# Merging two mask products, reading tokens from PSUM, moving a division to GpSimd, and giving a scheduler the flag `port_shared` and one higher cost figure, in a hybrid attention layer

## The chip, the cores and the metric

The kernel runs on the 8 cores of one Trainium2 chip (two dies, cores 0 to 3 and 4 to 7). Each core does the whole layer for 2048 of the 16384 tokens. The metric is the device time of the slowest core in microseconds (us). Runs come in states: a slow state with one or both dies at a lower clock is left out of every comparison. The span is first to last instruction.

## The reference

One decoder layer: attention in three dilated groups and a pooled branch, both gated and merged, one output projection, then a gated feed-forward. The parts that the change touches:

```python
h = rms_norm(x, g_pre_mix); proj = h @ w_in          # q, k, v, u (256 wide), gates
q, k = apply_rope(q), apply_rope(k)
# per group (window, dilation) = (128,1), (512,4), (2048,16), four heads of 64 each:
p = where(valid, exp(s - m), 0); den = sum(p); out = (p @ v) / den    # banded mask
# the groups are combined by their denominators: o = sum(num_g) / sum(den_g)
# pooled branch, group g of 64 channels, windows 2, 4, 8, 16:
z = trailing_sum(u, w) / count - u                    # mean minus the token itself
y_pool = (z @ w_mix[g]) * scale
merged = gate_a * (o_attn @ w_proj_attn) + gate_p * (y_pool @ w_proj_pool)
x = x + rms_norm(merged @ w_out, ...)
# feed-forward: silu(h2 @ w_gate) * (h2 @ w_up) @ w_down, residual, about half of the time
```

## The kernel before

The kernel records its operations as nodes. A list scheduler in the host program then fixes the order of every engine before anything runs: it simulates the engines with a cost per operation, lets an engine take the ready operation with the best priority, and assigns buffers from rings as it goes.

The cost of a GpSimd operation, and the point at which a node may start:

```python
def op_cost(eng, method, outs, ins, kw):
    ...                                    # TensorE, ScalarE, VectorE cut
    return 0.17 + (0.0034 if strided else 0.0021) * n      # GpSimd, n elements a partition

def earliest(self, n):
    t = n.ready
    if n.dma:
        t = max(t, self.dma_free - self.BACKLOG)
    ...                                    # places in buffer rings cut
    return t
```

One tile of scores, for two heads: TensorE, exponential on ScalarE, then a mask product on VectorE for each head (128x512, bf16, both inputs in SBUF). There are 48 such tiles and two buffers for them (`PT`).

```python
def att_qk(pair, items, mask):
    pt, sb = PT.new(), sc2.new()
    ...                                    # matmuls into sb
    act.activation(out=pt[:, :, :], in_=sb[:, :, :], func=AF.Exp, scale=0.125)
    for hh in range(2):
        dve.tensor_tensor(out=pt[:, hh, :], in0=pt[:, hh, :], in1=masks[:, mask, :], op=ALU.mult)
    return pt
```

The end of an attention block, for each of four token blocks and two head pairs: numerators `val` and denominators `den` come from PSUM, the reciprocal is an exponential of minus a logarithm, and VectorE multiplies:

```python
for o_, i_, hh in ((val[lo, :], lo, 0), (val[hi, :], hi, 1), (den[lo, :], hi, 0), (den[hi, :], lo, 1)):
    dve.tensor_tensor(out=o_, in0=ob[i_, hh, :], in1=acc[i_, s, 2 * pair + hh, :], op=ALU.add)
act.activation(out=den[:, :], in_=den[:, :], func=AF.Ln)
act.activation(out=den[:, :], in_=den[:, :], func=AF.Exp, scale=-1.0)
dve.tensor_tensor(out=oT2[...] rearranged, in0=val[...], in1=den[...], op=ALU.mult)
```

The pooled branch: the token values go from PSUM into an SBUF buffer `uX`, in front of which the last 16 columns of the block before are copied; GpSimd builds trailing sums by shifted additions; VectorE scales them and subtracts the token:

```python
for c in range(2):
    X = uX[c]
    dve.tensor_copy(out=X[:, 0:16], in_=uh[:, c, :] if s == 0 else X[:, 512:528])
    b = r1.new()                                   # one PSUM bank of the filling ring
    mm8(b[:, :], ...)
    act.activation(out=X[:, 16:UL], in_=b[:, :], func=AF.Copy)
for c in range(2):
    X = uX[c]
    shift_add(uY, X, 1); shift_add(uZ, uY, 2)      # GpSimd; two more when c == 1
    for p0, Sx in ((0, uY), (64, uZ)):
        p = slice(p0, p0 + 64)
        dve.scalar_tensor_tensor(out=zT[p, :], in0=Sx[p, 16:UL], scalar=invw[p, c:c + 1],
                                 in1=X[p, 16:UL], op0=ALU.mult, op1=ALU.subtract)
        ...                                        # first 16 columns of block 0 cut
```

GpSimd also does the rotary embedding's additions (`q`, `k` from the products `rt`, which VectorE forms with one operand in PSUM) and issues weight transfers. Meanwhile TensorE fills its time between attention tiles with the projections of the next block.

The softmax here doesn't subtract the row's maximum and nothing guards it: scores larger than these inputs give would overflow.

Of the kernel before, what the change touches and what calls it, by code (L numbers as in the profile page):

```python
# [8 lines left out]
AF = mybir.ActivationFunctionType  # L9
# [96 lines left out]
class Node:  # L106
    __slots__ = ("idx", "eng", "items", "outs", "ins", "deps", "succ", "cost", "prio", "dma", "sem", "vts", "start", "finish", "tick", "nin", "ready", "table", "prev")
# [17 lines left out]
class Eng:  # L125
# [16 lines left out]
    def call(self, method, *args, after=(), **kw):  # L142
        n = self.open
        if n is None:
            n = self.prog.node(self)
        outs, ins = [], []
        for i, a in enumerate(args):
            if isinstance(a, (bass.AP, VAP)):
                (outs if i == 0 else ins).append(a)
        for k, a in kw.items():  # L150
            if isinstance(a, (bass.AP, VAP)):
                (outs if k in ("out", "accum_out") else ins).append(a)
        n.items.append((method, args, kw))
        n.outs += outs
        n.ins += ins
        n.deps.update(a.idx for a in after if a is not None)
        n.cost += op_cost(self.name, method, outs, ins, kw)
        if method == "activation":
            t = TABLES.get(kw["func"])
            if t:  # L160
                n.table = t
        if self.open is None:
            self.prog.close(n)
        return n
# [61 lines left out]
def op_cost(eng, method, outs, ins, kw):  # L226
# [21 lines left out]
    return 0.17 + (0.0034 if strided else 0.0021) * n  # L248


class Prog:
# [42 lines left out]
    def node(self, eng):  # L294
        n = Node()
        n.idx = len(self.nodes)
        n.eng = eng
        n.items, n.outs, n.ins = [], [], []
        n.deps, n.succ = set(), []
        n.cost, n.dma, n.sem, n.table = 0.0, 0, None, None  # L300
        n.prio = n.idx + self.bias
        n.vts = []
        self.nodes.append(n)
        return n
# [140 lines left out]
    def earliest(self, n):  # L445
        t = n.ready
        if n.dma:
# [10 lines left out]
    def schedule(self):  # L458
# [13 lines left out]
        self.dma_free = 0.0  # L472
        self.order = []
        import bisect
        while len(self.order) < len(nodes):
# [39 lines left out]
            e.free = t + cost  # L515
            if n.dma:
# [128 lines left out]
def build_program():  # L645
# [292 lines left out]
    for d, w in todo:  # L938
        pool.dma(d, w, dsem("d_w01_"), after=[sp_x[-1]])
# [16 lines left out]
    def att_qk(pair, items, mask):  # L956
# [9 lines left out]
        for hh in range(2):  # L966
            dve.tensor_tensor(out=pt[:, hh, :], in0=pt[:, hh, :], in1=masks[:, mask, :], op=ALU.mult)
# [39 lines left out]
    def att(s):  # L1007
# [40 lines left out]
        for pair in range(2):  # L1048
# [7 lines left out]
            for o_, i_, hh in ((val[lo, :], lo, 0), (val[hi, :], hi, 1), (den[lo, :], hi, 0), (den[hi, :], lo, 1)):  # L1056
# [4 lines left out]
            dve.tensor_tensor(out=oT2[s % 3][:, pair, :].rearrange("p (j rho) -> p rho j", rho=4), in0=val[:, :].rearrange("p (rho j) -> p rho j", rho=4),  # L1061
                              in1=den[:, :].rearrange("p (rho j) -> p rho j", rho=4), op=ALU.mult)


    def pooled(s, r1):
        for c in range(2):
            X = uX[c]
            dve.tensor_copy(out=X[:, 0:16], in_=uh[:, c, :] if s == 0 else X[:, 512:528])
            b = r1.new()
            mm8(b[:, :], lambda k: wu[:, c, k, :], lambda k: hT[:, k, s * 512:(s + 1) * 512])  # L1070
            act.activation(out=X[:, 16:UL], in_=b[:, :], func=AF.Copy)

# [3 lines left out]
        for c in range(2):  # L1076
            X = uX[c]
            shift_add(uY, X, 1)
# [4 lines left out]
            for p0, Sx in ((0, uY), (64, uZ)):  # L1083
                p = slice(p0, p0 + 64)
                dve.scalar_tensor_tensor(out=zT[p, :], in0=Sx[p, 16:UL], scalar=invw[p, c:c + 1], in1=X[p, 16:UL], op0=ALU.mult, op1=ALU.subtract)
                if s == 0:
                    dve.tensor_tensor(out=Sx[p, 16:32], in0=Sx[p, 16:32], in1=invc[p, 16 * c:16 * c + 16], op=ALU.mult)
                    dve.tensor_tensor(out=zT[p, 0:16], in0=Sx[p, 16:32], in1=X[p, 16:32], op=ALU.subtract)
# [223 lines left out]
```

## Time and profile before

| | before |
|---|---|
| timed, median of 3 (range) | 1035.83 us (1034.78 to 1103.5) |
| profiled span, slowest core | 1022.7 us |
| TensorE / VectorE / GpSimd busy | 930.7 / 420.4 / 352.7 us |

I split the span by what TensorE does: up to its first attention scores; from there to the first gate matmul of the merge; from there to the first feed-forward matmul; the rest. Busy times by stretch, kernel before, core 5 (start and end; length, then busy time and instructions of TensorE, its weight loads, VectorE, ScalarE and GpSimd; granted clock; DMA share; GB/s):

```profile
0.00:149.20 149.20, 113.36 (x832) 76.11 (x832) 87.96 (x143) 85.30 (x160) 66.99 (x55) 0.95 0.71 189
149.20:308.00 158.80, 139.88 (x1390) 87.00 (x1390) 134.79 (x188) 80.54 (x109) 76.67 (x51) 0.97 0.21 39
308.00:547.60 239.60, 220.14 (x1165) 101.46 (x1164) 110.47 (x134) 103.32 (x157) 123.97 (x136) 0.98 0.46 109
547.60:1022.70 475.10, 457.35 (x2140) 207.91 (x2136) 87.23 (x109) 77.26 (x131) 85.07 (x109) 0.99 0.43 93
```

The length less TensorE's busy time is its gap: 35.8, 18.9, 19.5 and 17.8 us, 92 us in all. In the second stretch VectorE is busy for 134.8 of 158.8 us.

### The profile page before, as it was taken

How to read it: one execution, taken by the hardware profiler on the slowest of the kernel's cores; microseconds unless marked ns; L12 is line 12 of the kernel's file. 1: busy time of each engine (PE TensorE's matmuls, PEld its weight loads, DVE VectorE, ACT ScalarE, POOL GpSimd, SP SyncE). 2: the span in 40 equal slices, each digit the busy share in tenths (PEclk: the TensorE clock that was granted, in tenths of full speed). 3: DMA queues.
4: the chain of work that ended last, by engine and by line, in shares of the span. 5: the costliest groups of instructions: out<-in, count | busy, mean ns of one | idle time of the engine just before them, and what ended most of it. 6: DMA issues, size and time to landing. Idle time of an engine off the chain costs nothing.

```text
span 1022.7 us, 15344 instructions; the slowest of 8 cores (1018.5 to 1022.7 us)
## 1 busy us (share of the span) xinstructions
PE 930.7 (91%) x5520; PEld 472.5 (46%) x5520; DVE 420.4 (41%) x573; ACT 346.4 (34%) x556; POOL 352.7 (34%) x350
## 2 busy tenths in 40 slices
PE   2779898989787988999989999999999999999993
PEld 2346585556453443444444444444444444444441
DVE  5668448679998343433455211211112121121111
ACT  4686437645343242422766111111101111111110
POOL 1528445344757512333886110111332000001232
PEclk9899999999999989999999999999999999999997
DMA  8868711220061635331777667663323444430321
GB/s 234 261 188 217 172 30 43 31 54 1 1 114 22 99 59 121 62 62 22 208 263 225 117 116 124 119 109 62 124 104 122 83 79 69 80 62 1 124 83 41
DMA packets 30778, 105.02 MB, mean 103 GB/s; under 512 B 3952, under 2 KB 3952, under 8 KB 30704
## 3 DMA queue, kind: packets, MB, share of 16 engines
q0 software_dynamic: 14432, 45.65, 26.9%
q1 hardware_dynamic: 15984, 58.33, 17.1%
q8 instruction: 45, 0.74, 0.3%
q14 instruction: 29, 0.24, 0.1%
q10 hardware_dynamic: 288, 0.06, 0.1%
HBM read 132.90 MB, written 16.78 MB: 146 GB/s over the span
## 4 chain that ended last, share of the span: by engine, by line
PE 72%; DVE 9%; issue 7%; POOL 6%; ACT 5%; DMA 1%; DVEq 0%; POOLq 0%; ACTq 0%; SPq 0%
PE ps L596 63%; PE ps L594 9%; DVE PT_75_117 L594 2%; ACT xsb_53_95 L594 1%; DVE PT_74_116 L594 1%; DVE rt_72_114 L594 1%; DVE zT_134 L594 1%; DVE rt_73_115 L594 1%; DMA xst_37_79<-xo 1%; POOL x1b_101_143 L594 1%; POOL x1b_102_144 L594 1%; DVE hTh_69 L594 1%; POOL x1b_103_145 L594 1%; ACT junk_55_97 L594 1%; ACT PT_75_117 L594 0%
## 5 line engine op out<-in xcount | busy, mean ns | idle before, releaser
L596 PE MATMUL ps<-wdna_155,ffT_154 128*128 128x512 bf16 x512 | 115.7, 379 | 0.0
L596 PE MATMUL ps<-hT_68,wgu_109_151 128*128 128x512 bf16 x420 | 100.4, 379 | 0.0
L596 PE MATMUL ps<-hT_68,wgu_110_152 128*128 128x512 bf16 x420 | 100.4, 379 | 0.0
L596 PE MATMUL ps<-hT_68,wgu_111_153 128*128 128x512 bf16 x392 | 93.7, 379 | 0.0
L596 PEld LDWEIGHTS ps<-wdna_155,ffT_154 128*128 128x128 bf16 x512 | 50.1, 98 | 60.4
L596 PEld LDWEIGHTS ps<-hT_68,wgu_109_151 128*128 128x128 bf16 x420 | 41.0, 98 | 49.3
L596 PEld LDWEIGHTS ps<-hT_68,wgu_110_152 128*128 128x128 bf16 x420 | 41.0, 98 | 49.1
L596 PEld LDWEIGHTS ps<-hT_68,wgu_111_153 128*128 128x128 bf16 x392 | 38.4, 98 | 46.2
L596 PE MATMUL ps<-hT_68,wgs_76_118 128*128 128x512 bf16 x224 | 56.3, 393 | 2.9 <-ACT tg_80_122 L594 1.8
L596 PE MATMUL ps<-hT_68,wgs_77_119 128*128 128x512 bf16 x224 | 53.5, 379 | 2.1 <-ACT tg_81_123 L594 1.0
L594 DVE TENSOR_TENSOR ffT_154<-ps,sa_115_157 128x512 bf16<-128x512 f32 x30 | 20.7, 691 | 79.2 <-PE ps L594 79.2
L594 DVE TENSOR_TENSOR ffT_154<-ps,sa_116_158 128x512 bf16<-128x512 f32 x29 | 20.1, 692 | 78.4 <-PE ps L594 78.4
L594 DVE TENSOR_TENSOR ffT_154<-ps,sa_117_159 128x512 bf16<-128x512 f32 x29 | 20.1, 691 | 77.1 <-PE ps L594 77.1
L594 ACT ACTIVATE sa_115_157<-ps 128x512 f32<-128x512 f32 x30 | 17.9, 598 | 80.1 <-PE ps L594 80.1
L594 ACT ACTIVATE sa_116_158<-ps 128x512 f32<-128x512 f32 x29 | 17.3, 597 | 80.8 <-PE ps L594 80.8
L594 ACT ACTIVATE sa_117_159<-ps 128x512 f32<-128x512 f32 x29 | 17.3, 597 | 78.0 <-PE ps L594 78.0
L594 DVE TENSOR_TENSOR PT_75_117<-PT_75_117,masks_44 128x512 bf16<-128x512 bf16 x48 | 39.6, 864 | 8.6 <-ACT PT_75_117 L594 8.5
L594 ACT ACTIVATE junkd_107_149<-ps 128x1024 bf16<-128x1024 f32 x18 | 18.3, 1016 | 73.2 <-PE ps L594 73.1
L594 DVE SCALAR_TENSOR_TENSOR tg_80_122<-tg_80_122,ps 128x512 f32<-128x512 f32 x32 | 22.0, 689 | 46.8 <-ACT tg_80_122 L594 44.1
L596 PE MATMUL ps<-wdnb_156,ffT_154 128*128 128x512 bf16 x160 | 39.8, 379 | 0.0
L594 DVE SCALAR_TENSOR_TENSOR tg_81_123<-tg_81_123,ps 128x512 f32<-128x512 f32 x32 | 22.0, 687 | 40.4 <-ACT tg_81_123 L594 40.3
L594 ACT ACTIVATE junkd_108_150<-ps 128x1024 bf16<-128x1024 f32 x14 | 14.2, 1017 | 69.4 <-PE ps L594 69.4
(499 smaller groups left out, 1821.6 us busy)
## 6 DMA issues: line engine op xcount, KB each, us to landing
wgu_109_151<-wgu POOLq DMA_DIRECT2D x15, 512.0 KB, 5.8
wgu_110_152<-wgu POOLq DMA_DIRECT2D x15, 512.0 KB, 5.8
wgu_111_153<-wgu POOLq DMA_DIRECT2D x14, 512.0 KB, 5.7
wgs_76_118<-wg POOLq DMA_DIRECT2D x8, 512.0 KB, 5.3
wgs_77_119<-wg POOLq DMA_DIRECT2D x8, 512.0 KB, 6.1
wdna_155<-wdn POOLq DMA_DIRECT2D x8, 512.0 KB, 8.6
tab_70_112<-tab SPq DMA_DIRECT2D x6, 512.0 KB, 6.0
tab_71_113<-tab SPq DMA_DIRECT2D x6, 512.0 KB, 6.1
```

The lines of the kernel that those rows point to most:

```text
L594: e.ops.append(lambda q, m=method, a=a, k=k, s=sem.sem, v=step: getattr(q, m)(*a, **k).then_inc(s, v))
L596: e.ops.append(lambda q, m=method, a=a, k=k: getattr(q, m)(*a, **k))
```

## The change

The intent: take work off VectorE in the attention stage, keep it out of GpSimd's way, and let the scheduler know that a GpSimd instruction and a VectorE instruction with two inputs in SBUF hold each other up. In the trace of the kernel before, core 5, a VectorE multiply of this form took 4.88 us beside two GpSimd additions and 1.30 us with GpSimd idle; a rotary addition of GpSimd took up to 2.88 us beside such VectorE instructions, and at most 2.17 us beside those that read one operand from PSUM. "Shared port" is my name for this, in the diff and below; the traces show the waiting, not a port. One cost figure of the scheduler changes as well, that of GpSimd operations on rearranged data.

```diff
+def port_shared(eng, outs, ins):
+    return eng == "vector" and sum(not type(peek(a).tensor).__name__.startswith("PSum") and nelem(peek(a)) > 1 for a in ins) > 1
 ...
-    return 0.17 + (0.0034 if strided else 0.0021) * n
+    return 0.17 + (0.0040 if strided else 0.0021) * n
 ... # in earliest(); port_free is set when such a VectorE node is placed
+        if n.port:
+            t = max(t, self.pool.free)
+        elif n.eng is self.pool and not n.dma:
+            t = max(t, self.port_free)
 ... # in att_qk()
-        for hh in range(2):
-            dve.tensor_tensor(out=pt[:, hh, :], in0=pt[:, hh, :], in1=masks[:, mask, :], op=ALU.mult)
+        dve.tensor_tensor(out=pt[:, :, :], in0=pt[:, :, :], in1=fap(masks[:, mask, :], [(0, 2), (1, 512)]), op=ALU.mult)
 ... # in att(): denominators are added before numerators, and
-            dve.tensor_tensor(out=oT2[...], in0=val[...], in1=den[...], op=ALU.mult)
+            pool.tensor_tensor(out=oT2[...], in0=val[...], in1=den[...], op=ALU.mult)
 ... # in pooled(): one loop over c in place of two, u = the token's PSUM bank
-            dve.tensor_copy(out=X[:, 0:16], in_=uh[:, c, :] if s == 0 else X[:, 512:528])
+            pool.tensor_copy(out=X[:, 0:16], in_=uh[:, c, :] if s == 0 else X[:, 512:528])
-                dve.scalar_tensor_tensor(..., in1=X[p, 16:UL], op0=ALU.mult, op1=ALU.subtract)
+                dve.scalar_tensor_tensor(..., in1=u[p, :], op0=ALU.mult, op1=ALU.subtract)
```

The cut parts are the bookkeeping of the new flag, the first 16 columns of block 0, and a renamed semaphore in a loop that runs no times.

More of the change, by code (lines that the diff above doesn't have):

```diff
@@ L106 @@
 class Node:
-    __slots__ = ("idx", "eng", "items", "outs", "ins", "deps", "succ", "cost", "prio", "dma", "sem", "vts", "start", "finish", "tick", "nin", "ready", "table", "prev")
+    __slots__ = ("idx", "eng", "items", "outs", "ins", "deps", "succ", "cost", "prio", "dma", "sem", "vts", "start", "finish", "tick", "nin", "ready", "table", "prev", "port")
 class Proc:
@@ L157, in call @@
         n.cost += op_cost(self.name, method, outs, ins, kw)
+        n.port |= port_shared(self.name, outs, ins)
         if method == "activation":
@@ L302, in node @@
         n.vts = []
+        n.port = False
         self.nodes.append(n)
@@ L472, in schedule @@
         self.dma_free = 0.0
+        self.port_free = 0.0
         self.order = []
@@ L515, in schedule @@
             e.free = t + cost
+            if n.port:
+                self.port_free = e.free
             if n.dma:
@@ L937, in build_program @@
     sp.dma(masks[:, :, :], masks_d[:, :, :], dsem("d_masks"), after=[sp_x[-1]])
-    for d, w in todo:
-        pool.dma(d, w, dsem("d_w01_"), after=[sp_x[-1]])
+    for i, (d, w) in enumerate(todo):
+        pool.dma(d, w, dsem("d_w01x%d" % i), after=[sp_x[-1]])
     for g in range(4):
@@ L1055, in att @@
             lo, hi = slice(0, 64), slice(64, 128)
-            for o_, i_, hh in ((val[lo, :], lo, 0), (val[hi, :], hi, 1), (den[lo, :], hi, 0), (den[hi, :], lo, 1)):
+            for o_, i_, hh in ((den[lo, :], hi, 0), (den[hi, :], lo, 1), (val[lo, :], lo, 0), (val[hi, :], hi, 1)):
                 dve.tensor_tensor(out=o_, in0=ob[i_, hh, :], in1=acc[i_, s, 2 * pair + hh, :], op=ALU.add)
@@ L1060, in att @@
             act.activation(out=den[:, :], in_=den[:, :], func=AF.Exp, scale=-1.0)
-            dve.tensor_tensor(out=oT2[s % 3][:, pair, :].rearrange("p (j rho) -> p rho j", rho=4), in0=val[:, :].rearrange("p (rho j) -> p rho j", rho=4),
-                              in1=den[:, :].rearrange("p (rho j) -> p rho j", rho=4), op=ALU.mult)
+            pool.tensor_tensor(out=oT2[s % 3][:, pair, :].rearrange("p (j rho) -> p rho j", rho=4), in0=val[:, :].rearrange("p (rho j) -> p rho j", rho=4),
+                               in1=den[:, :].rearrange("p (rho j) -> p rho j", rho=4), op=ALU.mult)
     def pooled(s, r1):
-        for c in range(2):
-            X = uX[c]
-            dve.tensor_copy(out=X[:, 0:16], in_=uh[:, c, :] if s == 0 else X[:, 512:528])
-            b = r1.new()
-            mm8(b[:, :], lambda k: wu[:, c, k, :], lambda k: hT[:, k, s * 512:(s + 1) * 512])
-            act.activation(out=X[:, 16:UL], in_=b[:, :], func=AF.Copy)
         def shift_add(dst, src, k):
@@ L1077, in pooled @@
             X = uX[c]
+            pool.tensor_copy(out=X[:, 0:16], in_=uh[:, c, :] if s == 0 else X[:, 512:528])
+            u = r1.new()
+            mm8(u[:, :], lambda k: wu[:, c, k, :], lambda k: hT[:, k, s * 512:(s + 1) * 512])
+            act.activation(out=X[:, 16:UL], in_=u[:, :], func=AF.Copy)
             shift_add(uY, X, 1)
@@ L1084, in pooled @@
                 p = slice(p0, p0 + 64)
-                dve.scalar_tensor_tensor(out=zT[p, :], in0=Sx[p, 16:UL], scalar=invw[p, c:c + 1], in1=X[p, 16:UL], op0=ALU.mult, op1=ALU.subtract)
+                dve.scalar_tensor_tensor(out=zT[p, :], in0=Sx[p, 16:UL], scalar=invw[p, c:c + 1], in1=u[p, :], op0=ALU.mult, op1=ALU.subtract)
                 if s == 0:
                     dve.tensor_tensor(out=Sx[p, 16:32], in0=Sx[p, 16:32], in1=invc[p, 16 * c:16 * c + 16], op=ALU.mult)
-                    dve.tensor_tensor(out=zT[p, 0:16], in0=Sx[p, 16:32], in1=X[p, 16:32], op=ALU.subtract)
+                    dve.tensor_tensor(out=zT[p, 0:16], in0=Sx[p, 16:32], in1=u[p, 0:16], op=ALU.subtract)
             b = r1.new()
```

## The prediction

> **What bounds the kernel now.** I read the engine table and the 40-slice picture first, then the waits of TensorE, then the timeline of VectorE and GpSimd where TensorE has gaps.
>
> ```profile
> PE 930.7 (91%) x5520; PEld 472.5 (46%) x5520; DVE 420.4 (41%) x573; ACT 346.4 (34%) x556; POOL 352.7 (34%) x350
> ...
> PE   2779898989787988999989999999999999999993
> PEld 2346585556453443444444444444444444444441
> DVE  5668448679998343433455211211112121121111
> ```
>
> TensorE is the bound: 930.7 of 1022.7 us, and its row shows 9 through the whole feed-forward half. A change of VectorE's work can only win back TensorE's gaps. VectorE's row shows where that is possible: the 7, 9, 9, 9, 8 in slices 9 to 13, the attention stage. Busy time by stretch (start and end, length, then each engine's busy time, granted clock, DMA share, GB/s):
>
> ```profile
> 163.00:228.00 65.00, 56.65 (x614) 36.36 (x613) 48.44 (x69) 38.72 (x49) 28.78 (x19) 0.95 0.25 50
> 228.00:316.00 88.00, 76.14 (x654) 45.11 (x652) 84.33 (x115) 35.93 (x54) 49.79 (x34) 0.98 0.18 34
> 316.00:330.00 14.00, 10.15 (x60) 4.09 (x59) 10.78 (x13) 4.49 (x6) 10.24 (x9) 0.88 0.23 39
> 330.00:425.00 95.00, 87.96 (x469) 40.05 (x470) 40.14 (x61) 35.08 (x51) 32.59 (x33) 0.96 0.47 86
> ```
>
> TensorE's gaps are 65 - 56.65 = 8.4, then 11.9, 3.9 and 7.0 us: 31 us that this change can touch. The others (36 us before 125 us, which wait on loads and on the input norm; 6 in the output projection; 18 at the end) it leaves alone. From 228 to 316 us VectorE works 84.3 of 88 us, so there it, not TensorE, sets the pace. TensorE's waits from 163 to 330 us say on what (total, times, longest):
>
> ```profile
> PE ps L596 <- DVE PT_75_117 L594: 7.0, 5, 2.3
> PE ps L596 <- DVE PT_74_116 L594: 4.6, 4, 2.2
> PE ps L594 <- DVE zT_134 L594: 4.1, 2, 2.9
> PE ps L596 <- DVE rt_73_115 L594: 2.7, 2, 1.8
> ```
>
> The mask of the probabilities (PT) and the pooled difference (zT). Why VectorE is late shows in the timeline of its own and of GpSimd's instructions around 304 us (start, length):
>
> ```profile
> 303.89 4.88 DVE L594 TENSOR_TENSOR oT_2_84_126<-val_67,den_135 128x512 bf16<-128x512 f32 x1
> ```
> ```profile
> 303.42 2.13 POOL L594 TENSOR_TENSOR q_1_65_107<-rt_72_114 128x512 bf16<-128x512 f32 x1
> 305.49 2.10 POOL L594 TENSOR_TENSOR q_1_65_107<-rt_73_115 128x512 bf16<-128x512 f32 x1
> ```
>
> The same VectorE multiply takes 1.30 us when GpSimd is idle (five of its eight). Here it spans both GpSimd operations and ends 1.2 us after the second: it was **held**. Rotary products, which read one operand from PSUM, keep 0.68 us whatever GpSimd does. So of 420 us much is holding. I take each group's busy time less its undisturbed length, read from timeline rows with no GpSimd work beside them: masks 39.6 + 31.3 = 70.9 us in 96 instructions, a pair 0.755 undisturbed, 48 x 0.755 = 36.2, held 34.7; divisions 16.1 - 8 x 1.30 = 5.7; pooled differences 16.2 - 16 x 0.745 = 4.3; the 16-column copies into uX 4.7 - 8 x 0.16 = 3.4. Together 48 us.
>
> [...] the copies, one input, were held as well (1.79 against 0.16 us). [...] The records here show windows at 0.5 near 191, 229, 297, 331 and 372 us, six of 3.41 us in all, so fewer gaps may also give back clock.
>
> **The change part by part.**
> 1. Mask of two heads in one op. [...] 48 x 0.065 = 3 us of VectorE, some 1.5 in the dense stretch. The mask is repeated with a zero step on the outer dimension, the inner step stays one[...].
> 2. Pooled differences read the tokens from PSUM: one SBUF input, so the 4.3 us of holding goes, and the op goes from 0.745 to about 0.69 (a gate op of that form with one PSUM input has 0.69). It leaves GpSimd free as well. The price: the token bank, of four that feed the filling matmuls, is kept from the matmul through two or four GpSimd adds (1.1 to 1.4 us each) and two differences, some 4 to 8 us instead of 0.6. The rotary products need pairs of these banks. I charge 1 us.
> 3. Division on GpSimd: VectorE loses 16.1 us, GpSimd gains 8 x 2.1 = 17 (the rearranged 128x512 there measure 2.0 to 2.3, plain ones 1.26 to 1.31; this one is rearranged on the output). The uX copies go too: 4.7 us off VectorE, about 1.6 on GpSimd. Denominators are added first, so the logarithm starts 1.4 us earlier, which about pays for the slower multiply.
> 4. The scheduler charges the shared port: it puts PSUM operations in front while GpSimd is busy. It does not change the machine: where only a mask is ready, the mask still waits. The order of instructions built from both kernels shows 350 lines of difference on TensorE, none on the sync queue; the first third is only slightly reordered. The renamed semaphore does nothing, as that list is empty by then.
>
> VectorE's load from 228 to 316 us: 84.3 less five divisions (12.2), four pooled differences' holding (2.8), copies (2), masks (1.5) is 66, below TensorE's 76. But the **shared port** takes over as neighbour: GpSimd 46.0 us without its transfer issues, plus 5 x 2.1 and 1 for copies, plus 21 masks x 0.69 = 14.5, gives 72 us that cannot overlap, against 65 now (union of both engines' port operations in the timeline). Port 72 and TensorE 76 in one stage, in fixed order and with only two PT buffers, will not mesh perfectly. I give back half of the 11.9: 6 us. From 163 to 228, where most waits are masks behind GpSimd's rotary adds and nothing is taken off the port, 40% of 8.4: 3.4. From 316 to 330: 1.5. From 330 to 425, where the pooled differences cost TensorE 2.3: 1.5. Clock: one of six half-clock windows less, 1.5 us. Less 1 for the bank. Sum 3.4 + 6 + 1.5 + 1.5 + 1.5 - 1 = 12.9 us.
>
> **The rivals.**
> (a) GpSimd and the port become the bound: the masks are then held longer behind 17 us of new GpSimd work. For it: the 72 us above, and GpSimd now also carries the division that the merge waits for. Against: pooled differences leave the port. Gain 0 to 5 us, time 1031 to 1036.
> (b) The pooled bank blocks the filling matmuls: only four banks serve them, and two may be held at once. TensorE would wait on zT and on bank releases. Time 1030 to 1038.
> (c) The scheduler's better knowledge gets nearly all: 31 us of gaps and up to 10 us of half clock (six windows, 1.7 us each) are there; 25 us or more would be 1010 or lower. Against: a static order, two PT buffers.
> (d) All was hidden anyway, time 1033 to 1037: half of VectorE's 420 us lies in stretches where TensorE has no gap. But the four waits above, 18 us on VectorE directly, speak against no gain at all.
>
> **Range and chances.** The timed median before is 1035.83 us, 13 above the profiled span; I take the gain from it: 1035.8 - 12.9 = 1023. Low is 27 us of gain, 1009; high is none, 1036. Two per cent is below 1015.1, a gain of 20.7 or two thirds of all reachable gaps: 0.22. Slower by over 2% needs (a) and (b) together and worse: 0.02. Within: 0.76.
>
> **What would show it right or wrong.** Right: VectorE's busy time falls from 420 to about 375 (16 divisions, 5 copies, 3 masks, 5 pooled, the rest holding), GpSimd rises to about 370; merged masks undisturbed at 0.69; pooled differences near 0.69 always; TensorE's gaps from 163 to 425 us fall from 31 to 18 or so; waits of TensorE on zT shrink most. Wrong: [...] masks held for longer than 34.7 us in total; TensorE waiting for banks that uX or zT free; GpSimd's multiply over 2.5 us; or fewer half-clock windows making the gain much larger than the gaps. Before 160 us I expect no change beyond 2 us.

## The result, and the profile after

| | before | after |
|---|---|---|
| median of the timed runs | 1035.46 us (4 runs) | 1021.94 us (4 runs, two of them slow) |
| fast runs | 1034.78, 1035.1, 1035.83 | 1009.24, 1009.56 |
| profiled span, slowest core | 1022.7 us | 1007.7 us |

The ratio is 0.975, interval 0.9722 to 0.9779: faster by over 2%. It is the mean time of one kernel's fast runs over that of the other's in the same rounds, so not quite the ratio of the medians above. At 0.975, 1035.8 us become about 1010: a gain of some 26 us where 12.9 were forecast.

The cores view of the kernel after, profiled run (span and mean granted clock; cores 2, 3 and 5):

```profile
core 2: 990.8 us, clock 0.984
core 3: 988.9 us, clock 0.984
core 5: 1007.7 us, clock 0.957
```

Cores 2 and 3 are 15 us faster than the six others (1005.1 to 1007.7 us, clock 0.955 to 0.957, among them cores 0 and 1 of the same die) with the same program. Busy times by stretch, kernel after, first core 5, then core 2 (the columns are those of the stretches above):

```profile
40.00:202.00 162.00, 155.81 (x1222) 104.53 (x1223) 93.30 (x141) 96.64 (x166) 76.55 (x55) 0.81 0.47 119
```
```profile
40.00:202.00 162.00, 148.57 (x1361) 102.10 (x1377) 102.95 (x152) 105.95 (x177) 85.62 (x61) 0.98 0.53 128
```

In this window core 5's clock averaged 0.81, and it got fewer matmuls done (from 100 to 140 us one of 128x512 took 436 ns, on core 2 379 ns): its clock records show 0.8125 (13/16) from 46.9 to 208.3 us, and all six slow cores of this run have such a stretch of 162 us. On this chip most executions of every kernel had at least one pair of cores (0-1, 2-3, 4-5 or 6-7) in that state. It cost the kernel before about 10 us (1032.8 against 1022.3 for its cores at full clock) and the kernel after 15. It is why the timed median before stood 13 us above its profiled span, which had no such pair (1.6 of the 13 us are the usual distance from span to time: the profiled run was timed at 1024.27). On the three other chips used later it was nearly absent: there the kernel before took 1024.2 to 1025.5 us, and the kernel after, run again unchanged, 993.35.

So I compare **the median span of cores at full clock** (mean clock 0.972 or more): **before 1021.8 us** (186 cores of 28 runs, 1017.3 to 1025.2; 1021.6 to 1022.3 on each of four chips), **after 990.6** (12 cores) on the first chip and **989.3** (28 cores) on another. The change is worth 31 to 32 us.

The profile page of the kernel after, engine table and the slices of VectorE and granted clock:

```profile
PE 941.1 (93%) x5520; PEld 483.0 (48%) x5520; DVE 379.4 (38%) x509; ACT 349.2 (35%) x558; POOL 364.9 (36%) x366
...
DVE  5667625658767434332544121121112112111111
...
PEclk9888888899999999999999999999999999999997
```

VectorE fell from 420.4 to 379.4 us, its stretch of 7, 9, 9, 9, 8 became 5, 8, 7, 6, 7, and the clock row shows the 8s of the throttled start. TensorE's 941 us are inflated by that clock: core 3, at full clock, has 918.2 us for the same 5520 matmuls. The same stretches as before, from the unchanged repeat on core 0, all cores at full clock:

```profile
0.00:139.40 139.40, 108.69 (x816) 74.10 (x816) 87.90 (x143) 84.42 (x158) 67.20 (x55) 0.96 0.78 202
139.40:282.70 143.30, 131.47 (x1355) 84.94 (x1355) 99.91 (x131) 80.33 (x110) 81.70 (x59) 0.98 0.20 36
282.70:513.60 230.90, 221.08 (x1215) 104.41 (x1216) 105.61 (x127) 106.72 (x160) 131.74 (x145) 1.00 0.56 118
513.60:988.80 475.20, 457.34 (x2139) 207.91 (x2136) 87.23 (x109) 77.19 (x131) 85.02 (x109) 0.98 0.51 94
```

| stretch | length before, after | TensorE's gap before, after | TensorE busy, change |
|---|---|---|---|
| to the first scores | 149.2, 139.4 | 35.8, 30.7 | -4.7 |
| to the first gate | 158.8, 143.3 | 18.9, 11.8 | -8.4 |
| to the feed-forward | 239.6, 230.9 | 19.5, 9.8 | +0.9 |
| rest | 475.1, 475.2 | 17.8, 17.9 | 0.0 |

These two cores differ by 33.9 us: 21.8 of gaps and 12.1 of busy time, for the same number of matmuls (5520 records each; about 50 of them moved from the first two stretches into the third). Of the 12.1, the clock explains most. Windows of 3.41 us at half clock fell from ten to five up to the feed-forward, and one costs at most half its length, 1.7 us, so up to 8.5. In the kernel before, each of the five stretches of half clock after 149 us (one of them two windows long) follows a window in which TensorE was busy for only 15 to 50% of the time, so fewer gaps and more clock go together. The rest I can't attribute.

TensorE's waits over the attention and the merge, 149 to 420 us, first the kernel before on core 5, then the kernel after on core 2, which had full clock (total, times, longest):

```profile
PE ps L596 <- DVE PT_75_117 L594: 7.6, 7, 2.3
PE ps L594 <- DVE zT_134 L594: 6.4, 4, 2.9
PE ps L596 <- DVE PT_74_116 L594: 4.6, 4, 2.2
```
```profile
PE ps L610 <- ACT PT_75_117 L608: 4.3, 9, 1.3
PE ps L610 <- DVE rt_73_115 L608: 2.7, 2, 2.3
PE ps L610 <- DVE PT_74_116 L608: 2.1, 3, 0.7
PE ps L610 <- issue: 1.6, 10, 0.2
PE ps L610 <- DVE PT_75_117 L608: 1.5, 4, 0.9
```

The waits on VectorE's masks went from 12.2 to 3.6 us, and the wait on the pooled difference left the top of the list. The groups behind them, kernel after, core 2 (busy us, mean ns; then the idle time before):

```profile
L608 DVE TENSOR_TENSOR PT_75_117<-PT_75_117,masks_44 128x1024 bf16<-128x1024 bf16 x24 | 30.0, 1252 | 12.1 <-ACT PT_75_117 L608 12.1
L608 DVE TENSOR_TENSOR PT_74_116<-PT_74_116,masks_44 128x1024 bf16<-128x1024 bf16 x24 | 23.4, 975 | 5.4 <-ACT PT_74_116 L608 5.2
L608 DVE SCALAR_TENSOR_TENSOR zT_134<-uZ_133,small_45,ps 64x512 bf16<-64x512 f32 x8 | 6.0, 754 | 0.3
L608 DVE SCALAR_TENSOR_TENSOR zT_134<-uY_132,small_45,ps 64x512 bf16<-64x512 f32 x8 | 5.9, 735 | 0.5 <-PE ps L608 0.4
```

Mask products took 70.9 us before and take 53.4 now. Undisturbed, a merged one takes 0.68 to 0.69 us, so 48 x 0.685 = 32.9, and 20.5 us are holding, against 34.7. The pooled differences are never held any more, but the operation itself is no faster: 0.74 to 0.75 us.

### The profile page after: what moved, and what is told of

It reads as the page before. It is cut to its first block, busy times and chain, and to the rows that moved or that the text cites. A ratio compares the mean times of both kernels' runs of the same rounds, so it can differ in the third digit from the quotient of the medians.

```text
span 1007.7 us, 15210 instructions; the slowest of 8 cores (988.9 to 1007.7 us)
## 1 busy us (share of the span) xinstructions
PE 941.1 (93%) x5520; PEld 483.0 (48%) x5520; DVE 379.4 (38%) x509; ACT 349.2 (35%) x558; POOL 364.9 (36%) x366
## 4 chain that ended last, share of the span: by engine, by line
PE 82%; DVE 4%; POOL 4%; issue 4%; ACT 2%; DMA 1%; SPq 0%; POOLq 0%; DVEq 0%; ACTq 0%
PE ps L610 73%; PE ps L608 10%; DMA xst_40_82<-xo 1%; DVE PT_75_117 L608 1%; ACT xsb_53_95 L608 1%; POOL x1b_103_145 L608 1%; POOL x1b_102_144 L608 1%; DVE PT_74_116 L608 1%; DVE rt_73_115 L608 1%; POOL x1b_101_143 L608 0%; DVE zT_134 L608 0%; POOL x1b_104_146 L608 0%; POOL q_33_75 L608 0%; DVE val_67 L608 0%; DVE x1b_102_144 L608 0%
## 5 line engine op out<-in xcount | busy, mean ns | idle before, releaser
L608 ACT ACTIVATE sa_115_157<-ps 128x512 f32<-128x512 f32 x30 | 17.9, 598 | 80.2 <-PE ps L608 80.2
L608 DVE SCALAR_TENSOR_TENSOR tg_81_123<-tg_81_123,ps 128x512 f32<-128x512 f32 x32 | 22.0, 688 | 47.8 <-ACT tg_81_123 L608 44.7
L608 POOL DMA_DIRECT2D wgu_109_151<-wgu x15 | 8.0, 536 | 81.3 <-PE ps L608 81.3
L608 POOL DMA_DIRECT2D wgu_110_152<-wgu x15 | 8.2, 544 | 80.7 <-PE ps L608 80.7
```

The source lines that it names most:

```text
L608: e.ops.append(lambda q, m=method, a=a, k=k, s=sem.sem, v=step: getattr(q, m)(*a, **k).then_inc(s, v))
```

## The experiments

Theories at the start. **Holding**: each VectorE operation with two inputs in SBUF that starts while GpSimd works waits until GpSimd is done (the multiply of 4.88 us against 1.30), so the fewer such operations, the better; the gain comes from masks and pooled differences. **Scheduler**: the gain comes from the order, that is, from the flag for the port or from the cost figure. **Division**: the gain comes from what GpSimd took over. All kernels gave correct results. The gaps to the kernel after (989.3 to 990.6 us) are stated for medians of cores at full clock.

### One part undone at a time

Four kernels, each the kernel after with one part back as it was, on the first chip.

m_port: the scheduler knows neither the port nor the new cost.

```diff
-    return eng == "vector" and sum(...) > 1
+    return False and eng == "vector" and sum(...) > 1
-    return 0.17 + (0.0040 if strided else 0.0021) * n
+    return 0.17 + (0.0034 if strided else 0.0021) * n
```

> The change without its fourth part: the scheduler knows nothing of the shared port and keeps the old cost of rearranged GpSimd operations; the instructions are those of the changed kernel. Theory O (the order is what pays): nearly all of the 7 us before the first attention scores and over 10 us of the attention stage go; fast runs 1022 or more against 1009.7. Theory L (VectorE's and the port's load is what pays): 4 us or less are lost in the attention stage, fast runs 1010 to 1016, and the masks' held time stays near 20 us.

Measured: 997.2 us at full clock, a loss of 6.6; ratio to before 0.9805 (0.9781 to 0.983). On its cores at full clock the first scores start at 148.6 to 150.0 us, as before. Neither theory fits: O asked for more, L for less.

m_mask: two mask products again.

```diff
-        dve.tensor_tensor(out=pt[:, :, :], in0=pt[:, :, :], in1=fap(masks[:, mask, :], [(0, 2), (1, 512)]), op=ALU.mult)
+        for hh in range(2):
+            dve.tensor_tensor(out=pt[:, hh, :], in0=pt[:, hh, :], in1=masks[:, mask, :], op=ALU.mult)
```

> The change without its first part: two mask operations for each pair of heads. Undisturbed that is 48 x 0.07 = 3.4 us more of VectorE. Theory L: 2 to 4 us lost. Theory T or O: under 2 us. If merging is worth more than its 3.4 us, two operations must be held twice as often, which would show in over 25 us of held mask time against 19.5.

Measured: 1005.0 us at full clock, a loss of 14.4; ratio 0.98, interval 0.9675 to 0.9925 (two fast runs only, one of them with a throttled pair). Masks are held for 44 us (80.6 less 36.2), so two operations are held about twice as long, as the last sentence of the expectation asks.

m_psum: the pooled branch as before, in all of it: two loops, copies on VectorE, tokens from SBUF.

```diff
+        for c in range(2):
+            X = uX[c]
+            dve.tensor_copy(out=X[:, 0:16], ...); b = r1.new(); ...   # as in the kernel before
         for c in range(2):
             X = uX[c]
-            pool.tensor_copy(out=X[:, 0:16], ...); u = r1.new(); ...
-  in1=u[p, :], op0=ALU.mult, op1=ALU.subtract)
+  in1=X[p, 16:UL], op0=ALU.mult, op1=ALU.subtract)
```

> The change without its second part: the pooled differences read the tokens from SBUF again, the 16-column copies are VectorE's again. Theory L: 4 us of holding and 1.3 us of copies come back, and TensorE waits on the pooled differences again (6 us before): 4 to 8 us lost. Theory T or O: 3 us or less.

Measured: 1006.2 us, a loss of 15.6; ratio 0.988 (0.9861 to 0.99). The copies alone are held for 14.8 us (16.1 less 1.3).

m_div: the division back on VectorE, and the numerators added first again.

```diff
-            for o_, i_, hh in ((den[lo, :], hi, 0), (den[hi, :], lo, 1), (val[lo, :], lo, 0), (val[hi, :], hi, 1)):
+            for o_, i_, hh in ((val[lo, :], lo, 0), (val[hi, :], hi, 1), (den[lo, :], hi, 0), (den[hi, :], lo, 1)):
-            pool.tensor_tensor(out=oT2[...]
+            dve.tensor_tensor(out=oT2[...]
```

> The change without its third part: division on VectorE again, values added before denominators. Theory L: VectorE takes back 8 x 1.3 us and whatever is held, most of it in the dense stretch, so 6 to 10 us are lost. Theory T (once VectorE is off the path, each part alone is spare): 3 us or less are lost. Theory O: 3 us or less as well, as the scheduler plans around it.

Measured: 986.8 us at full clock, a gain of 3.8. Its timed runs mostly had throttled pairs (median 1006.77); the one run with all cores at full clock took 991.26.

What follows: 6.6 + 14.4 + 15.6 - 3.8 = 32.8, about the whole, but partly by chance, as the table of all runs will show. The mask and the pooled branch lose most when undone, two to seven times what theory L's sums said; the division, which was to lose 6 to 10 us, loses nothing. Each of these kernels was also reordered by the scheduler, so the next runs keep the order where they can.

### Why one mask product is worth more than the 3 us it saves

g_mask: two products again, but recorded as one node with the cost of the merged one. The order of every engine is then that of the kernel after (compared instruction by instruction: no difference but the split product).

```diff
-        dve.tensor_tensor(out=pt[:, :, :], in0=pt[:, :, :], in1=fap(masks[:, mask, :], [(0, 2), (1, 512)]), op=ALU.mult)
+        with dve.group() as n_:
+            for hh in range(2):
+                dve.tensor_tensor(out=pt[:, hh, :], in0=pt[:, hh, :], in1=masks[:, mask, :], op=ALU.mult)
+            n_.cost = 0.12 + 0.00060 * 1024
```

> Every engine's order is that of the changed kernel, with the merged mask replaced by two operations back to back that the scheduler places as one. Compared on the cores at full clock, where the changed kernel spans 990 us and the kernel with the merge undone and all rescheduled 1005. Theory H (each operation with two SBUF inputs can be held by itself, so two are held more): held mask time rises from 20 to 30 us or more, and the span to 998 to 1004. Theory U (merging saves only its undisturbed 48 x 0.07 us): 991 to 994, held time about 20 us. Theory G (what the undone merge lost was the scheduler's placing): 990 to 992.

Measured: 1001.5 us, a loss of 10.9 to 12.2; ratio 0.9785 (0.9745 to 0.9825). The timeline shows why. VectorE, then GpSimd, of g_mask at the first masks (start, length; in brackets idle time before):

```profile
143.95 0.42 DVE L610 TENSOR_TENSOR PT<-PT,masks 128x512 bf16<-128x512 bf16 x1
144.28 2.33 DVE L608 TENSOR_TENSOR PT<-PT,masks 128x512 bf16<-128x512 bf16 x1
```
```profile
144.18 2.15 POOL L608 TENSOR_TENSOR q<-rt 128x512 bf16<-128x512 f32 x1 [4.13 <-DVE rt L608]
```

The same place in the kernel after (the repeat), VectorE, then GpSimd:

```profile
142.92 0.68 DVE L608 TENSOR_TENSOR PT<-PT,masks 128x1024 bf16<-128x1024 bf16 x1
```
```profile
143.15 4.95 POOL L608 TENSOR_TENSOR q<-rt 128x512 bf16<-128x512 f32 x2 [4.12 <-DVE rt L608]
```

With two products GpSimd's addition comes in between: the first product ends after 0.42 us, the addition runs, and the second product lasts 2.33 us until the addition is done at 146.33. With one product it is over after 0.68 us, and GpSimd's first two additions, whose instructions began at 143.15, take 4.95 us in place of some 4.3. As far as these lines go, **each product is held by itself, and whichever engine came second waited for the other's whole instruction**: the second product took 2.33 us, and GpSimd's pair of additions some 0.65 us more than alone, about the 0.68 us of the merged product. Every product less is a place less where GpSimd can step in. Groups of g_mask (the first line is the second product of each pair, the second the first product), then the group of the repeat:

```profile
L608 DVE TENSOR_TENSOR PT<-PT,masks 128x512 bf16<-128x512 bf16 x48 | 39.4, 821 | 0.0
L610 DVE TENSOR_TENSOR PT<-PT,masks 128x512 bf16<-128x512 bf16 x48 | 35.5, 739 | 14.9 <-ACT PT L608 14.6
```
```profile
L608 DVE TENSOR_TENSOR PT<-PT,masks 128x1024 bf16<-128x1024 bf16 x48 | 52.9, 1115 | 17.5 <-ACT PT L608 17.3
```

Of 74.9 us, 48 x 0.755 = 36.2 are work and 38.7 holding; merged, 20. Little of this waiting moves to GpSimd: over the whole run it is busy for 362.6 us in g_mask and 365.7 in the kernel after, with the same instructions, so 3 us of the 18.7 that VectorE is held less. TensorE's wait for the masks from 138 to 425 us, g_mask, then the repeat:

```profile
PE ps L610 <- DVE PT L608: 12.8, 14, 1.8
```
```profile
PE ps L610 <- DVE PT L608: 3.4, 6, 1.0
```

a_mask: the merged product alone, on the kernel before.

```diff
-        for hh in range(2):
-            dve.tensor_tensor(out=pt[:, hh, :], in0=pt[:, hh, :], in1=masks[:, mask, :], op=ALU.mult)
+        dve.tensor_tensor(out=pt[:, :, :], in0=pt[:, :, :], in1=fap(masks[:, mask, :], [(0, 2), (1, 512)]), op=ALU.mult)
```

> The kernel before with the merged mask alone. The parts taken out of the changed kernel one at a time lose 6, 14, 16 and -4 us, together the whole 32. Theory A (the parts add up): 1022 less 10 to 15 us, 1007 to 1012, held mask time from 34.7 to about 20 us. Rival T (VectorE is still bound by the others, so alone it does little): 1017 or more.

Measured: 1003.2 us against 1021.8, a gain of 18.6; ratio 0.9823 (0.9805 to 0.9841). Holding of masks falls from 34.7 to 18.0 us, although pooled differences and divisions are then held more (10.8 and 6.6 us, against 4.3 and 5.7). The first scores start at 147.0 to 150.2 us, as before, so all of it is won later. The 18.6 include whatever the new order is worth; g_mask, at unchanged order, gives 11 to 12.

### Which part of the pooled branch pays

x_tok: the 512-column differences read the tokens from SBUF again; the PSUM bank is still recorded as read and the flag for the port is not set, so order and life of the bank stay those of the kernel after.

```diff
-  in1=u[p, :], op0=ALU.mult, op1=ALU.subtract)
+  in1=X[p, 16:UL], op0=ALU.mult, op1=ALU.subtract, also=[u[p, :]], known=False)
```

> Every engine's order and every bank's life is that of the changed kernel; the 16 pooled differences alone read the tokens from SBUF, so they have two SBUF inputs again. Cores at full clock, against 990. Theory H: the pooled differences are held by 4 us or more, and their waits come back to TensorE: 993 to 998. Theory C (the 15 us that undoing this part lost are those of the 16-column copies, which there stood held for 15 us on VectorE): under 2 us lost, 990 to 992.

Measured: 993.0 us, a loss of 2.4 to 3.7; the differences are held for 3.2 us in all; ratio 0.9699 (0.9651 to 0.9747). With the life of the bank the same, the price that I charged for that (1 us) is neither shown nor refuted.

c_copy: only the copies of 16 columns back on VectorE.

```diff
-            pool.tensor_copy(out=X[:, 0:16], ...)
+            dve.tensor_copy(out=X[:, 0:16], ...)
```

> The changed kernel with the eight 16-column copies back on VectorE, nothing else. Undisturbed they are 8 x 0.16 = 1.3 us. Theory C: a copy with one SBUF input is held by GpSimd as a mask is, and the scheduler does not know it; 8 us or more of held copies, and 995 to 1004 on the cores at full clock. Theory H: 2 us or less lost.

Measured: 994.4 us, a loss of 3.8 to 5.1; ratio 0.9724 (0.9683 to 0.9765).

xc_loop: both, in the new loop: copies on VectorE, tokens from SBUF.

```diff
-            pool.tensor_copy(out=X[:, 0:16], ...)
+            dve.tensor_copy(out=X[:, 0:16], ...)
-  in1=u[p, :], op0=ALU.mult, op1=ALU.subtract)
+  in1=X[p, 16:UL], op0=ALU.mult, op1=ALU.subtract)
```

> The changed kernel with the two parts of the pooled change undone together, copies on VectorE and tokens from SBUF, but in the changed kernel's loop: one channel half after the other. Alone they cost 4 and 2 us; undoing the whole part with its loop cost 16. Theory X (holding of both adds up to more): 1000 to 1006. Theory R (the other 10 us are the old loop, which computes both token halves first): 994 to 998.

Measured: 1006.7 us, a loss of 16 to 17, the same as m_psum (1006.2); ratio 0.9853 (0.9837 to 0.9868). So no value of the order of the loops is seen, and the two remaining halves are worth far more together than the 2.4 and 3.8 us they cost apart. The group of the copies in xc_loop, then in c_copy:

```profile
L608 DVE COPY uX<-uX 128x16 f32<-128x16 f32 x6 | 12.7, 2124 | 0.0
```
```profile
L608 DVE COPY uX<-uX 128x16 f32<-128x16 f32 x6 | 5.0, 840 | 0.1
```

A copy of 16 columns takes 0.16 us undisturbed; here one takes 2.12 on average. One of them, at the end of attention in xc_loop, on VectorE, then GpSimd's instructions there:

```profile
300.29 5.10 DVE L608 COPY uX<-uX 128x16 f32<-128x16 f32 x1
```
```profile
301.16 4.18 POOL L608 TENSOR_TENSOR k<-rt 128x512 bf16<-128x512 f32 x2
```

The copy ends at 305.39, 0.05 us after GpSimd's two rotary additions, and VectorE did nothing else for 5 us. So a copy, with one input, was held too: 5.10 us here against 0.16. The flag `port_shared` counts inputs and so does not see it. Why the two together lose so much more than apart is settled only in part: with the differences in SBUF they carry the flag, so the scheduler changes the order on GpSimd and VectorE, and in that order the copies meet longer GpSimd work (2.12 against 0.84 us each). x_tok, which kept the order, does not show what that reordering alone costs.

### The division

d_den: the division on VectorE, but denominators still added first.

```diff
-            pool.tensor_tensor(out=oT2[...]
+            dve.tensor_tensor(out=oT2[...]
```

> The changed kernel with the division alone back on VectorE; denominators are still added first. Theory D (moving it costs: it lengthens GpSimd's work, which the rotary results wait on): 984 to 988 against 990. Theory M (the gain of the earlier run came from adding values first): 990 or more.

Measured: 990.8 us and 993.48 timed, against 989.3 and 993.35 of the kernel after on the same chip: no difference. Moving the division is neutral; on VectorE it is held for 0.2 us in all in this order. So the 3.8 us of m_div come from the other order of additions or from luck; no run tells which. On GpSimd the division is cheaper than the 2.1 us that I charged. Groups of GpSimd, kernel after, core 2: two groups of rotary additions, then a group of divisions:

```profile
L608 POOL TENSOR_TENSOR k_1_62_104<-rt_73_115 128x512 bf16<-128x512 f32 x2 | 4.3, 2132 | 0.0
L608 POOL TENSOR_TENSOR k_1_59_101<-rt_73_115 128x512 bf16<-128x512 f32 x2 | 2.6, 1288 | 0.3 <-DVE rt_73_115 L608 0.3
L608 POOL TENSOR_TENSOR oT_0_82_124<-val_67,den_135 128x512 bf16<-128x512 f32 x4 | 5.8, 1441 | 3.2 <-PE ps L608 2.0 <-ACT den_135 L608 1.1
```

The first group reads its input with a step of four float32 elements, the second in order; the division reads in order and only writes with a step (undisturbed 1.34 to 1.37 us; 1.49 on average over the eight in the repeat). So in this trace a *read* with a 16-byte step cost 2.13 against 1.29 us, 65% more, and the write with a step had no such price.

### What the scheduler's knowledge is worth

s_cost: the cost of 0.0040 stays, but the scheduler does not know the port.

```diff
-    return eng == "vector" and sum(...) > 1
+    return False and eng == "vector" and sum(...) > 1
```

> The changed kernel with the new cost for rearranged GpSimd operations but a scheduler that is blind to the port. Blind with the old cost spans 996 on the cores at full clock and its first attention scores start at 148.6 us, as before; the changed kernel has 990 and 141.6. Theory K (the early 7 us come from the cost): scores start at 142 or sooner and 991 or less. Theory P (they come from the knowledge of the port): scores start at 147 or later, 995 to 998.

Measured: 987.8 us and 990.62 timed; ratio 0.9645 (0.9598 to 0.9692). Without the knowledge of the port the kernel is at least as fast as with it. m_port differs from s_cost in the cost alone and takes 997.2 us, so the difference, 9.4 us, is the cost's. In these two orders the flag does not lessen the holding that it was made for: masks are held for 15.5 us in s_cost and 20 in the kernel after.

b_cost: the kernel before with nothing changed but the cost.

```diff
-    return 0.17 + (0.0034 if strided else 0.0021) * n
+    return 0.17 + (0.0040 if strided else 0.0021) * n
```

> The kernel before with one figure of the change: the scheduler's cost of a rearranged GpSimd operation 0.0040 instead of 0.0034 us an element. No instruction changes, only order. Theory K (that figure is worth the early 7 us): first attention scores at 142 us or sooner against 148.6, span 1012 to 1017 on cores at full clock against 1022. Rival (the early gain needs the other parts): scores after 146, span over 1019.

Measured: 1006.3 us against 1021.8: a gain of 15.5 from one digit of a cost model; ratio 0.9867 (0.9849 to 0.9885). Its first scores start at 139.0 us in place of 149, so 10 us are won before the stage that the change was aimed at. Where they are won shows between 108 and 121 us, core 0 of the kernel before, then of b_cost (columns as in the stretches above):

```profile
108.00:121.00 13.00, 9.63 (x58) 5.42 (x57) 7.34 (x12) 5.73 (x14) 1.72 (x1) 0.87 0.76 151
```
```profile
108.00:121.00 13.00, 12.32 (x99) 10.32 (x98) 10.47 (x17) 3.45 (x9) 10.04 (x9) 1.00 0.90 196
```

GpSimd's rotary additions on the same two cores, the first after its pause (in brackets):

```profile
119.28 1.94 POOL L594 TENSOR_TENSOR k_34_76<-rt_72_114 128x512 bf16<-128x512 f32 x1 [12.70 <-DVE rt_72_114 L594]
```
```profile
110.96 8.00 POOL L594 TENSOR_TENSOR k<-rt 128x512 bf16<-128x512 f32 x4 [6.19 <-DVE rt L594]
```

The old order leaves a hole: GpSimd stands idle for 12.7 us, and TensorE gets 58 matmuls done in 13 us. With the new figure there are 99. The traces of all cores at full clock divide by the figure alone, whatever else was changed: 56 to 66 matmuls in this window with 0.0034 (before, a_mask, m_port), 94 to 107 with 0.0040 (12 kernels), and 89 to 100 and 72 to 99 with 0.0037 and 0.0043 of the next two runs.

c_0037 and c_0043: the kernel after with two other figures.

```diff
-    return 0.17 + (0.0040 if strided else 0.0021) * n
+    return 0.17 + (0.0037 if strided else 0.0021) * n      # c_0043: 0.0043
```

> The changed kernel with 0.0037 us an element for a rearranged GpSimd operation. These measure 2.0 to 2.3 us, so 0.0037 (2.06) and 0.0040 (2.22) are both fair, 0.0034 (1.91) is low. Theory K (a true figure pays): scores start at 140 to 143 us, span within 4 us of 990. Theory J (any change of order shakes the start by some us either way): scores anywhere from 138 to 150, span 986 to 1000.

> The same with 0.0043 (2.37 us, above what is measured). Theory K: as with 0.0040, scores at 140 to 143, or a little later, span 988 to 994. Theory J: scores from 138 to 150, span 986 to 1000.

Measured, on the chip of the repeat: 998.2 us (ratio 0.9786, 0.9769 to 0.9804) and 990.8 us (0.9719, 0.9703 to 0.9734), with 989.3 for 0.0040. The first scores start at 143.3, 139.8 and 139.4 us on core 0 (143.1 to 147.0, 139.8 to 144.4 and 139.2 to 141.3 over the eight cores), and masks are held for 33.1 us at 0.0037 (66.0 less 32.9). The gain is not a smooth function of the figure, and theory K (a true figure pays) fails: rearranged GpSimd reads of 512 elements that nothing disturbs take 1.93 to 2.17 us (kernel before, 120 to 149 us), so 0.0037, which says 2.06, is the truest of the four figures, and it is 8.9 us worse than 0.0040, which says 2.22. It fills the hole before 121 us as the others do, but in its order the masks meet GpSimd more often. Theory J (any change of order shakes the times) is the one that fits.

best1: s_cost and m_div together, the two parts whose undoing had not hurt.

```diff
-    return eng == "vector" and sum(...) > 1
+    return False and eng == "vector" and sum(...) > 1
-            for o_, i_, hh in ((den[lo, :], hi, 0), ...
+            for o_, i_, hh in ((val[lo, :], lo, 0), ...
-            pool.tensor_tensor(out=oT2[...]
+            dve.tensor_tensor(out=oT2[...]
```

> The changed kernel without its two parts that lose: division back on VectorE, scheduler blind to the port, the rest (merged mask, tokens from PSUM, copies on GpSimd, new cost) kept. If the two add up, 990 less 4 less 2: 984 on cores at full clock. If they cure the same trouble, 986 to 988; if the division needs the knowledge of the port, over 990.

Measured: 993.2 us, ratio 0.9728 (0.9713 to 0.9744): 5 to 6 us worse than either alone. The third theory, over 990, forecast the number, and the trace has something of it: the divisions are held for 4.7 us here (15.1 less 10.4), against 0.2 in d_den, which has the flag. That is only a part of the 5 to 6 us. So differences of up to 9 us between two static orders (0.0037 against 0.0040 above is 8.9) can't be put down to the part that was edited; some of it is how instructions happen to meet.

### The kernel after once more

after_clean: unchanged, to have it on a chip without throttled pairs.

> The changed kernel unchanged, for comparison on one chip. On cores at full clock it spanned 990 us against 1022 before; if no pair of cores is held at a lower clock here, its time is 993 or so and the ratio to before 0.968.

Measured: 993.35 us, ratio 0.9697 (0.9679 to 0.9714); the median core took 989.3 us. Both s_cost (990.62 timed) and the undisturbed run of m_div (991.26) lie 0.2 to 0.3% below this, on other chips: within what the intervals leave open. No version was shown to beat the kernel after.

The comparisons between these kernels rest on the spans alone. Table of all runs, median span of the cores at full clock:

| kernel | us | kernel | us |
|---|---|---|---|
| before | 1021.8 | m_port | 997.2 |
| a_mask | 1003.2 | g_mask | 1001.5 |
| b_cost | 1006.3 | m_mask | 1005.0 |
| after | 990.6, 989.3 | m_psum | 1006.2 |
| s_cost | 987.8 | xc_loop | 1006.7 |
| m_div | 986.8 | x_tok | 993.0 |
| d_den | 990.8 | c_copy | 994.4 |
| best1 | 993.2 | c_0037, c_0043 | 998.2, 990.8 |

The parts do not add up. On the kernel before, the mask alone gains 18.6 and the cost alone 15.5, together more than the whole change. Yet m_psum, which has the mask, the cost, the flag and the division, takes 1006.2, about as much as either of the two alone; only with the pooled branch changed as well do they come to 990. The kernel before with mask and cost and nothing else was not run.

## Why the prediction was right or wrong

The direction was right, and so was the mechanism in the attention stage, with its sizes too small; of the 33.9 us by which the two profiled cores differ, 9.8 were won in a stage that the prediction left out. The time was 13 us too high, and faster by over 2% had been given 0.22.

- **Right**: TensorE is the bound, and only its gaps ahead of the feed-forward can be won; the rest moved by 0.1 us. VectorE went to 379.4 us ("about 375"), GpSimd to 364.9 ("about 370"), a merged mask to 0.68 to 0.69, the waits on zT nearly vanished. Rivals (a), (b) and (d) did not happen. Rival (c), "nearly all" of the gaps and half-clock windows, came closest, but not for its reason: no gain from the knowledge of the port is seen (s_cost).
- **Failed, the largest step**: "Before 160 us I expect no change beyond 2 us". The first scores came 7 to 10 us earlier. I had compared orders and called the first third "only slightly reordered", but did not ask what the new cost of GpSimd's rearranged operations does there. b_cost shows the same 10 us from the cost figure alone. I treated the figure as part of the flag for the port, and it was the part that mattered: it closed the hole of 12.7 us in front of 119 us.
- **Failed, a size**: the mask was priced as "48 x 0.065 = 3 us of VectorE, some 1.5 in the dense stretch". The 0.065 us a pair (0.755 less 0.69 for a merged mask) was my estimate, which no trace had shown by then. That saving was about right (0.755 to 0.685 us a pair, 3.4 us) and beside the point. At unchanged order the merged product is worth 11 to 12 us of span (g_mask), because it removes 48 places at which GpSimd can step in. I had measured the holding (34.7 us), yet took the merged product to be held as much as the pair.
- **Failed, a size**: the gaps. The terms 3.4, 6, 1.5 and 1.5 come to 12.4 us; the gaps from the first scores to the feed-forward shrank by 16.7, and 16.1 of them lie in the part that the terms cover. "I give back half of the 11.9" had no measurement behind it.
- **Failed, a size**: "one of six half-clock windows less, 1.5 us". Up to the feed-forward five of ten went, four of them between the first scores and the feed-forward, so up to 7 us. Shorter gaps paid twice, once as time and once as clock. (The places of the windows, 191 to 372 us, are 11.7 us too late, being counted from the trace's own zero and not from the first instruction; the count of six is right.)
- **Overcharged, no effect**: the division at 2.1 us on GpSimd; it measures 1.34 to 1.37 undisturbed and 1.49 on average, and its place makes no difference (d_den).
- **Wrong in detail**: pooled differences "from 0.745 to about 0.69" stayed at 0.745. That part still pays 15.6 us, with the copies, which I had valued at 4.7 us of VectorE's time rather than at what they delay.
- **A slip without effect**: "21 masks" in the sum for the port are 18 pairs (36 products from 228 to 316 us), so the port's 72 us are 70.
- **The base**: 1035.8 us held a pair of cores at the lower clock (a mean of 0.95 against 0.977 in the runs of the kernel before that were timed with m_port). The 13 us above the profiled span were visible, and I took the gain from them without asking what they were. Because the kernel after pays more for such a pair (15 against 10 us), the gain on that chip looks smaller (26 us) than on others (31).

In sum, on one core at full clock each: 5.1 us of gaps and 4.7 of busy time ahead of the scores, of which I expected none; 16.7 of gaps behind, where I expected 12.4; 7.5 less busy time behind, where I expected 1.5 of clock. The early part comes from the cost figure, as all runs show; but a truer figure as such is not what pays (c_0037), so that 0.0040 led to a good order in the later stages too may be luck.

## What to carry to other kernels

Count the instructions of VectorE that read from SBUF alone beside a busy GpSimd, not only their time. Here each could be held for a whole GpSimd instruction: 0.42 against 2.33 us for a mask product, 1.30 against 4.88 for a division, 0.16 against up to 5.10 for a copy of 16 columns. Fewer and larger ones, one operand in PSUM, and no small copies in SBUF were worth more than the VectorE time they take away: 11 to 12 us of span for the 3.4 us of the merged mask (g_mask), 15.6 for the pooled branch (m_psum), priced at 4.3 us of holding and 4.7 of copies. Where a static scheduler sets the order, change its cost figures alone before crediting an edit, and expect 5 to 10 us in 1000 of mere reshuffling in any comparison that lets the order move. Before taking a gain from a median, look at the clock of every core in it.
